# Delta-net stage of a hybrid trunk: later key and value transposes, pair scales on VectorE, E blocks fixed ahead of the KQ copies on GpSimd

## The chip, the cores and the metric

The kernel runs on one core of a Trainium2 chip. The metric is the device time of one execution in microseconds; the median of several runs is quoted. One execution was taken by the hardware profiler, and all rows below are from it. TensorE multiplies, VectorE (DVE), ScalarE (ACT) and GpSimd (POOL) do the rest, and SyncE's queue (SP) loads the weights.

## The reference

Two layers on x of 256 tokens by 1024, each h + ½·FFN_a, h + mixer, h + ½·FFN_b, with an RMSNorm before and behind each part. The mixer of layer 0 is a short gated convolution. That of layer 1 is a gated delta-net, cut to what matters here:

```
qkv, z, b, a = split(x @ w_in)
qkv = silu(causal_conv(qkv, conv_w))       # width 4, each channel by itself
q, k, v = split(qkv)                       # 8 key heads, 16 value heads of 128
q, k = l2norm(q), l2norm(k); beta = sigmoid(b)
g = -exp(a_log) * softplus(a + dt_bias)    # per head and token, then cumsum in a chunk of 64
a_ = strict_lower(k_beta @ k.T * decay)    # per chunk
t_inv = inverse(eye + a_)                  # unit lower triangular
u = t_inv @ v_beta; w = t_inv @ (k_beta * exp(g))
# over the chunks: v_new = u - w @ state; o = q_g @ state + qk @ v_new; the state is updated
o = rms_norm(o) * norm_w * silu(z);  y = o @ w_out
```

## The kernel before, in words

The 256 tokens are two tiles of 128. The kernel is a stream of weight units of 128x1024: each is loaded by SyncE into one of three buffers (raw), split on ScalarE into a high part (whi, `unit`, L119) and on VectorE into a low part (wlo, L121), eight of each in a pool, and used by three matmuls per product (high by high, high by low, low by high). Results of the projections go to four PSUM banks named mm; four others (acc) serve the small products. TensorE takes its instructions in program order. Work that isn't a projection lies in generators ("chains"). A ticker resumes them: every group of 24 matmuls of a projection (`stat_group`, two to a bank, for keys and values; `act_group`, one to a bank, for z) calls `tk.tick()` two or four times, and a chain that yields n is resumed n ticks later. So the constants KQ_WAIT, INV_WAIT, V_WAIT set where in the stream of matmuls a step of a chain is placed. The order on the other engines is made by the scheduler from the program, per engine and fixed; `tc.issue_after` pins an instruction behind another.

The delta-net stage (`gdn_proj`, about 690 to 880 us of the profile) goes so:

- The head slabs: gates a and b, and the first seven of the 16 key and query columns. `gates` (L530 to L537) makes beta, the log decay and its sums; `decays` makes the decay matrices (dec) with exponentials on ScalarE and masks on GpSimd (L559).
- The other columns of keys and queries. `conv` (L583) is one ScalarE operation that reads the bank, and three VectorE operations that read it again; `kq_raw` and `kq_silu` follow, then, one group of two key heads after the other, `kq_chain`: transposes on TensorE (L618), a copy, products KQ (L621), sums of squares (junk, kss, L630), scales (rk, dsc, nk, eq), KQ times its decay (L645), and copies of its 32x32 blocks into blk (L652).
- `invert`: a transpose on VectorE (L669), 62 small VectorE operations (L677, L679; they grow from 31 to 256 columns and shrink again), two more transposes (L681, L683). GpSimd copies the results into KQ (L689, 32 copies) and E (L699, L700), and TensorE puts the blocks together (L707 to L739).
- Three z groups (`z_group`, a bank per tile, then a SiLU into zs that empties it, L573), and four value groups, each of two pairs (`v_pair`): a bank of two heads, `conv` into yb, SiLU, a wait of V_WAIT ticks, transposes (L757) into another mm bank, scaled copies nv (L759). The last z group, the scan over the chunks and the output projection follow.

The order of the projections, and the pair's chain:

```
        for gi in range(NG - 1):
            z_group(gi)
        for gi in range(NG):
            v_group(gi)
        z_group(NG - 1)
```

Of the kernel before, what the change touches and what calls it, by code (L numbers as in the profile page):

```python
# [7 lines left out]
F32 = mybir.dt.float32  # L8
F32R = mybir.dt.float32r
AF = mybir.ActivationFunctionType  # L10
ALU = mybir.AluOpType
PSUM = bass.MemoryType.PSUM

P = 128
T = 256
NT = 2
# [5 lines left out]
NG = 4  # L22
# [7 lines left out]
NSMALL = 22  # L30
NBIG = 8
NROW = 3
KQ_WAIT = 3
INV_WAIT = 37
V_WAIT = 4
SCAN_WAIT = 2
ORD = "00111222"
GORD = "00012222"
# [11 lines left out]
def trunk_kernel(ctx: ExitStack, tc: tile.TileContext, x, norm_g, w_gu, w_dn, sc_in, sc_cw, sc_out,  # L50
# [425 lines left out]
    def gdn_proj(xh, xl, mid):  # L476
# [30 lines left out]
        def gates():  # L507
            def sm(name):
                return sp.tile([P, NT, NVH], F32, name=name, bufs=1)

            a, u, e, z, q = sm("ga"), sm("gb"), sm("gc"), sm("gd"), sm("ge")
            G.tensor_tensor(a, ba[:, :, NVH:], bc(dtb, NT), ALU.add)
            G.tensor_scalar(u, a, 0.0, -2.0, ALU.max, ALU.mult)
            G.tensor_tensor(e, a, u, ALU.add)
            first = S.activation(e, e, AF.Exp).ins
            with tc.issue_after(first):
                S.activation(al, al, AF.Exp)
            S.activation(beta, ba[:, :, 0:NVH], AF.Exp, scale=-1.0)

            V.tensor_scalar(z, e, 2.0, None, ALU.add)  # L520
            V.reciprocal(z, z)
            V.tensor_tensor(z, z, e, ALU.mult)
            V.tensor_tensor(u, z, z, ALU.mult)
            V.tensor_scalar(q, u, 1.0 / 19.0, None, ALU.mult)
            for k in (17, 15, 13, 11, 9, 7, 5, 3):
                V.scalar_tensor_tensor(q, q, 1.0 / k, u, ALU.add, ALU.mult)
            V.scalar_tensor_tensor(q, q, 1.0, z, ALU.add, ALU.mult)
            V.tensor_scalar(a, a, 0.0, None, ALU.max)
            V.scalar_tensor_tensor(q, q, 2.0, a, ALU.mult, ALU.add)
            V.scalar_tensor_tensor(g, q, -1.0, bc(al, NT), ALU.mult, ALU.mult)  # L530
            G.tensor_scalar(beta, beta, 1.0, None, ALU.add)
            V.reciprocal(beta, beta)
            pg = side_bank().rearrange("p a b -> p (a b)")[:, 0:2 * NVH].rearrange("p (t n) -> p t n", t=NT)
            PE.matmul(pg[:, 0, :], lhsT=tri_s, rhs=g[:, 0, :], start=True, stop=True)
            PE.matmul(pg[:, 1, :], lhsT=tri_u, rhs=g[:, 1, :], start=True, stop=True)
            S.activation(etail, pg[:, 0, :], AF.Exp)
            S.activation(eg, pg[:, 1, :], AF.Exp)  # L537

        def decays():
# [10 lines left out]
                gus.append(gu)  # L550
            while not convs:
                yield 1
            for gi in range(NG):
                for t in range(NT):
                    pd = side_bank()
# [30 lines left out]
                V.scalar_tensor_tensor(dst[:, j:], src[:, 0:T - j], cw[:, ch, 3 - j:4 - j],  # L586
                                       dst[:, j:], ALU.mult, ALU.add)

        raws, kq_time = {}, [0] * KD

        def kq_raw(kh, c, src):
            if kh not in raws:
                raws[kh] = slab([P, 2, T], F32, "kq")
            conv(raws[kh][:, c, :], src, c * KD + kh)
            if c == 1:
                if dec_done[0]:
                    kq_silu(kh, raws[kh])
                else:
                    convs.append((kh, raws[kh]))
# [5 lines left out]
        def kq_chain():  # L605

            for gi in range(NG):
# [23 lines left out]
                    yield 1  # L631
                while dec[1][gi] is None:
                    yield 1
                G.tensor_scalar(ss, ss, EPS, None, ALU.add)
                rk = sp.tile([P, NT, 2], F32, name="rk", bufs=2)
                V.reciprocal(rk, ss[:, :, 0, :])
                dd = small(f"dsc{gi}", 8).rearrange("p (t n) -> p t n", t=NT)
                for t in range(NT):
                    G.tensor_tensor(dd[:, t, :].rearrange("p (k v) -> p k v", k=2),
                                    beta[:, t, 4 * gi:4 * gi + 4].rearrange("p (k v) -> p k v", k=2),  # L640
                                    rk[:, t, :].unsqueeze(2).broadcast_to([P, 2, 2]), ALU.mult)
                for t in range(NT):
# [14 lines left out]
                w = small(f"wt{gi}", 4)  # L657
                G.tensor_tensor(w, etail[:, 4 * gi:4 * gi + 4], dd[:, 0, :], ALU.mult)
                Dsc[gi], nk[gi], eq[gi], wt[gi] = dd, n, q, w
                yield 1  # L660
            tk.start(invert())


# [3 lines left out]
        def invert():  # L667
# [14 lines left out]
            Yd = row("blk").rearrange("p (a b) -> p a b", a=B32)  # L682
            V.transpose(Yd.rearrange("p h i -> p i h"), X)  # L683
            T1 = row("blk").rearrange("p (a b) -> p a b", a=B32)
            for gi in range(NG):
                for t in range(NT):
                    for b in range(4):
                        r = slice(b * B32, (b + 1) * B32)
                        G.tensor_copy(KQ[gi][t][r, :, 0, r], Yd[r, 8 * gi + t:8 * gi + t + 7:2, :])  # L689
            yield INV_WAIT  # L690
            for half in range(2):
                hs = slice(16 * half, 16 * half + 16)
                gis = (2 * half, 2 * half + 1)
                E = {}
                for gi in gis:
                    E[gi] = slab([P, 8, 64], F32, "E64")
                    for b in range(2):
                        r = slice(b * B32, (b + 1) * B32)
                        G.tensor_copy(E[gi][r, :, r], Xd[r, 8 * gi:8 * gi + 8, :])  # L699
                    G.memset(E[gi][0:B32, :, B32:], 0.0)  # L700
                pt = side_bank().rearrange("p a (b c) -> p (a b) c", c=B32)
                for x in range(16):
                    ht = 16 * half + x
# [44 lines left out]
        def v_pair(gi, i, pt, tiles):  # L748
# [1 line left out]
            for j in range(2):  # L750
                conv(vc[:, j, :], pt[:, j, :], 16 + 4 * gi + 2 * i + j)
            silu(vc, vc)
            yield V_WAIT
            tp = ps.tile([P, NT, 2, P], F32, name="mm")
            for t in range(NT):
                for j in range(2):
# [134 lines left out]
        def head_tail(late):  # L891
            yield 1
            late()
            for kh, c in order[0:7]:
                kq_raw(kh, c, craw[kh][:, c, :])

        tk.start(head_tail(head_slabs([load_slab(gdn_h0, GSPLIT, GORD), load_slab(gdn_h1, GSPLIT, GORD[4:])], xh, xl, evac_head, mid, 0)))
# [158 lines left out]
```

## Time and profile before

| | us |
|---|---|
| runs, lowest, median, highest | 1125.82, 1127.42, 1130.31 |
| the profiled execution | 1128.42 |
| its span, first to last instruction | 1126.5 |
| TensorE busy in it | 1100.2 (98%) |
| VectorE, ScalarE, GpSimd busy | 749.9, 651.8, 88.8 |
| mean granted TensorE clock | 0.995 |

Busy time is the time in which an engine has an instruction under way; waits are what is left of the span. A start in the timeline counts from the span's beginning. Where an engine was idle before an instruction, the row says for how long and which instruction, of which engine and line, released it.

### The profile page before, as it was taken

How to read it: one execution, taken by the hardware profiler on the slowest of the kernel's cores; microseconds unless marked ns; L12 is line 12 of the kernel's file. 1: busy time of each engine (PE TensorE's matmuls, PEld its weight loads, DVE VectorE, ACT ScalarE, POOL GpSimd, SP SyncE). 2: the span in 40 equal slices, each digit the busy share in tenths (PEclk: the TensorE clock that was granted, in tenths of full speed). 3: DMA queues.
4: the chain of work that ended last, by engine and by line, in shares of the span. 5: the costliest groups of instructions: out<-in, count | busy, mean ns of one | idle time of the engine just before them, and what ended most of it. 6: DMA issues, size and time to landing. Idle time of an engine off the chain costs nothing.

```text
span 1126.5 us, 16842 instructions
## 1 busy us (share of the span) xinstructions
PE 1100.2 (98%) x6284; PEld 942.4 (84%) x6284; DVE 749.9 (67%) x1140; ACT 651.8 (58%) x1201; POOL 88.8 (8%) x167
## 2 busy tenths in 40 slices
PE   9999999999999999999999999889899999999997
PEld 6888887888788888788888877778899887888886
DVE  7776735687777663577765468768946557767543
ACT  6666535545556653556664358784587645666432
POOL 0100000000200000010000012110141212000000
PEclk9999999999999999999999999999999999999999
DMA  8755555656566565576555653327332355655552
GB/s 271 244 185 190 191 166 167 225 180 198 182 223 204 171 206 165 163 229 209 189 185 169 193 185 113 94 94 227 114 129 76 131 168 168 213 199 190 185 168 75
DMA packets 55955, 198.12 MB, mean 176 GB/s; under 512 B 6721, under 2 KB 7233, under 8 KB 55874
## 3 DMA queue, kind: packets, MB, share of 16 engines
q1 hardware_dynamic: 55728, 196.99, 54.2%
q8 instruction: 49, 0.80, 0.3%
q14 instruction: 32, 0.26, 0.1%
q10 hardware_dynamic: 146, 0.07, 0.0%
HBM read 195.99 MB, written 1.05 MB: 175 GB/s over the span
## 4 chain that ended last, share of the span: by engine, by line
PE 81%; DVE 7%; ACT 5%; DMA 3%; issue 2%; POOL 2%; SPq 0%; DVEq 0%; POOLq 0%; ACTq 0%
PE mm L298 27%; PE mm L301 14%; PE acc L324 7%; PE acc L325 7%; PE acc L323 7%; PE mm L221 3%; PE mm L222 3%; PE mm L225 3%; DVE wlo L121 2%; ACT whi L119 1%; ACT blk L652 1%; DVE kq L586 1%; PE mm L176 1%; ACT junk L147 1%; DMA raw<-in_w_gu 1%
## 5 line engine op out<-in xcount | busy, mean ns | idle before, releaser
L121 DVE TENSOR_TENSOR wlo<-raw,whi 128x1024 fp32r<-128x1024 f32 (+2 forms) x362 | 437.5, 1220 | 240.2 <-ACT whi L119 201.5
L119 ACT ACTIVATE whi<-raw 128x1024 fp32r<-128x1024 f32 (+2 forms) x362 | 376.1, 1051 | 224.3 <-PE acc L325 104.6
L298 PE MATMUL mm<-x,whi 128*128 128x512 f32 x1312 | 329.4, 393 | 0.0
L298 PEld LDWEIGHTS mm<-x,whi 128*128 128x128 f32 x1312 | 235.9, 189 | 42.4
L301 PEld LDWEIGHTS mm<-x,wlo 128*128 128x128 f32 x1312 | 179.0, 190 | 12.8
L301 PE MATMUL mm<-x,wlo 128*128 128x256 f32 x1312 | 182.9, 282 | 0.0
L323 PE MATMUL acc<-whi,hb 128*128 128x512 f32 x352 | 136.5, 388 | 0.0
L324 PE MATMUL acc<-wlo,hb 128*128 128x512 f32 x352 | 135.6, 385 | 0.3 <-DVE wlo L121 0.3
L325 PE MATMUL acc<-whi,hb 128*128 128x512 f32 x352 | 135.3, 385 | 0.0
L308 ACT ACTIVATE corr<-mm 128x256 f32<-128x256 f32 x164 | 61.2, 376 | 67.4 <-PE mm L301 65.6
L221 PE MATMUL mm<-whi,x 128*128 128x512 f32 (+1 forms) x240 | 94.4, 394 | 0.9 <-ACT x L178 0.7
L222 PE MATMUL mm<-wlo,x 128*128 128x512 f32 (+1 forms) x240 | 94.2, 393 | 0.7 <-DVE wlo L121 0.7
L225 PE MATMUL mm<-whi,x 128*128 128x512 f32 (+1 forms) x240 | 87.8, 389 | 0.2 <-DVE x L179 0.2
L324 PEld LDWEIGHTS acc<-wlo,hb 128*128 128x128 f32 x352 | 66.2, 188 | 13.8 <-DVE wlo L121 0.8
L323 PEld LDWEIGHTS acc<-whi,hb 128*128 128x128 f32 x352 | 66.2, 188 | 13.1
L325 PEld LDWEIGHTS acc<-whi,hb 128*128 128x128 f32 x352 | 66.1, 188 | 13.2
L154 POOL TENSOR_SCALAR rstd<-ss 128x1 f32<-128x1 f32 x24 | 12.3, 513 | 786.1 <-ACT junk L147 786.1
L278 PE MATMUL mm<-x,whi 128*128 128x256 f32 x200 | 59.7, 299 | 2.0 <-DVE kq L586 2.0
L279 PE MATMUL mm<-x,whi 128*128 128x256 f32 x200 | 58.4, 292 | 0.0
L280 PE MATMUL mm<-x,wlo 128*128 128x256 f32 x200 | 57.9, 289 | 0.0
L222 PEld LDWEIGHTS mm<-wlo,x 128*128 128x128 f32 x240 | 45.2, 188 | 11.2 <-DVE wlo L121 2.9
L221 PEld LDWEIGHTS mm<-whi,x 128*128 128x128 f32 x240 | 45.2, 188 | 11.1 <-ACT x L178 2.7
(216 smaller groups left out, 1238.3 us busy)
## 6 DMA issues: line engine op xcount, KB each, us to landing
raw<-in_w_gu SPq DMA_DIRECT2D x176, 512.0 KB, 4.2
raw<-in_w_dn SPq DMA_DIRECT2D x88, 512.0 KB, 3.6
raw<-in_sc_in SPq DMA_DIRECT2D x24, 512.0 KB, 4.1
raw<-in_gdn_z SPq DMA_DIRECT2D x16, 512.0 KB, 3.9
raw<-in_gdn_v SPq DMA_DIRECT2D x16, 512.0 KB, 4.2
raw<-in_gdn_out SPq DMA_DIRECT2D x16, 512.0 KB, 3.7
gamma<-in_norm_g SPq DMA_DIRECT2D x11, 512.0 KB, 5.4
raw<-in_gdn_a SPq DMA_DIRECT2D x9, 512.0 KB, 4.4
```

The costliest lines, as they stand in the source:

```text
L119: S.activation(hi[:, r], raw[:, r], AF.Copy)
L121: newest[0] = V.tensor_tensor(lo[:, r], raw[:, r], hi[:, r], ALU.subtract).ins
L221: PE.matmul(pt, lhsT=xh[:, t, k, :], rhs=hi, start=(k == 0), stop=False)
L222: PE.matmul(pt, lhsT=xh[:, t, k, :], rhs=lo, start=False, stop=False)
L225: PE.matmul(pt, lhsT=xl[:, t, j, :], rhs=part(j)[0], start=False, stop=(j == KD - 1))
L278: PE.matmul(ptile, lhsT=hi, rhs=h2, start=(k == 0), stop=False)
L298: PE.matmul(flat, lhsT=part(k, 0), rhs=xx[:, k].rearrange("p h t q -> p (h t q)"), start=(k == 0), stop=False)
L301: PE.matmul(flat[:, T:], lhsT=part(k, 1), rhs=xx[:, k, 0].rearrange("p t q -> p (t q)"), start=False, stop=(k == KD - 1))
L308: S.activation(c, pt[:, 1, :], AF.Copy)
L323: PE.matmul(o, lhsT=yh(c, t), rhs=hi[:, r], start=(c == 0), stop=False)
L324: PE.matmul(o, lhsT=yh(c, t), rhs=lo[:, r], start=False, stop=False)
L325: i = PE.matmul(o, lhsT=yl(c, t), rhs=hi[:, r], start=False, stop=(c == n - 1)).ins
```

## The change

Names and numbers only: KQ_WAIT goes from 3 to 5 ticks, the wait behind a key pair from 1 to 3 (PAIR_WAIT), V_WAIT from 4 to 9, 6, 4, 4 by value group, and the head's seven convolutions are issued four and then, three ticks later, three (CONV_WAIT). `kq_raw` counts the two parts of a key head in place of waiting for the second column. The sums of the gates (two matmuls, two exponentials) move from `gates` into `decays`, behind the first convolutions. The EPS addition and the scale dsc go from GpSimd to VectorE. In `invert`, `place(half)` issues for each half the E copies and zeros and then 16 KQ copies, in an order that is pinned; the second half is placed later.

```
-KQ_WAIT = 3
+KQ_WAIT = 5
+PAIR_WAIT = 3
-V_WAIT = 4
+V_WAIT = (9, 6, 4, 4)
+CONV_WAIT = 3
...
+        def gate_sums():
             pg = side_bank().rearrange("p a b -> p (a b)")[:, 0:2 * NVH].rearrange("p (t n) -> p t n", t=NT)
...
             while not convs:
                 yield 1
+            gate_sums()
...
             conv(raws[kh][:, c, :], src, c * KD + kh)
-            if c == 1:
+            parts[kh] += 1
+            if parts[kh] == 2:
...
-                G.tensor_scalar(ss, ss, EPS, None, ALU.add)
+                V.tensor_scalar(ss, ss, EPS, None, ALU.add)
...
-                    G.tensor_tensor(dd[:, t, :].rearrange("p (k v) -> p k v", k=2),
+                    V.tensor_tensor(dd[:, t, :].rearrange("p (k v) -> p k v", k=2),
...
-                yield 1
+                yield PAIR_WAIT
             tk.start(invert())
...
-            for gi in range(NG):
-                for t in range(NT):
-                    for b in range(4):
+            E, placed = {}, [None]
+
+            def place(half):
+
+                gis = (2 * half, 2 * half + 1)
+                for gi in gis:
+                    E[gi] = slab([P, 8, 64], F32, "E64")
+                    for b in range(2):
                         r = slice(b * B32, (b + 1) * B32)
-                        G.tensor_copy(KQ[gi][t][r, :, 0, r], Yd[r, 8 * gi + t:8 * gi + t + 7:2, :])
+                        with tc.issue_after(placed[0]) if placed[0] else nullcontext():
+                            G.tensor_copy(E[gi][r, :, r], Xd[r, 8 * gi:8 * gi + 8, :])
+                    with tc.issue_after(placed[0]) if placed[0] else nullcontext():
+                        last = G.memset(E[gi][0:B32, :, B32:], 0.0).ins
+                placed[0] = last
+                for gi in gis:
+                    for t in range(NT):
+                        for b in range(4):
+                            r = slice(b * B32, (b + 1) * B32)
+                            with tc.issue_after(placed[0]):
+                                last = G.tensor_copy(KQ[gi][t][r, :, 0, r], Yd[r, 8 * gi + t:8 * gi + t + 7:2, :]).ins
+                placed[0] = last
+
+            place(0)
             yield INV_WAIT
...
-                E = {}
-                for gi in gis:
-                    E[gi] = slab([P, 8, 64], F32, "E64")
...
+                if half:
+                    place(1)
...
             silu(vc, vc)
-            yield V_WAIT
+            yield V_WAIT[gi]
...
-            for kh, c in order[0:7]:
+            for i, (kh, c) in enumerate(order[0:7]):
+                if i == 4:
+                    yield CONV_WAIT
                 kq_raw(kh, c, craw[kh][:, c, :])
```

How the instructions stand, at three places. Numbers behind a name tell buffers apart; line numbers of the change are its own (SiLU L578 for L573, conv L589 and L591 for L584 and L586, projections L280 for L278).

ScalarE, from the last copies of the keys' blocks to the second value pair. Before (zs is the SiLU of a z bank, yb a value pair):

```order
L652 ACTIVATE blk_6238<-KQ_7222 32x4x32 x3
L119 ACTIVATE whi_7481<-raw_7479 128x1024 [waits DMAHW4_49,PE_49]
...
L573 ACTIVATE zs_7450<-mm_7425 128x512 [waits PE_49]
...
L573 ACTIVATE zs_7477<-mm_7452 128x512 [waits PE_49]
...
L573 ACTIVATE zs_7528<-mm_7503 128x512 [waits PE_49]
...
L573 ACTIVATE zs_7555<-mm_7530 128x512 [waits PE_49]
L119 ACTIVATE whi_7711<-raw_7709 128x1024 [waits DMAHW7_49,DVE_49]
L584 ACTIVATE yb_7645<-mm_7583,gcw_6224 128x256 [waits PE_49]
L584 ACTIVATE yb_7645<-mm_7583,gcw_6224 128x256 [waits DVE_49]
```

In the change:

```order
L658 ACTIVATE blk_6238<-KQ_7282 32x4x32 x3
L121 ACTIVATE whi_7563<-raw_7561 128x1024 [waits DMAHW2_49,PE_49]
...
L589 ACTIVATE yb_7637<-mm_7575,gcw_6224 128x256 [waits PE_49]
L589 ACTIVATE yb_7637<-mm_7575,gcw_6224 128x256 [waits DVE_49]
L578 ACTIVATE yb_7637<-yb_7637 128x512 [waits DVE_49,Activation_49]
...
L589 ACTIVATE yb_7722<-mm_7624,gcw_6224 128x256 [waits PE_49]
L589 ACTIVATE yb_7722<-mm_7624,gcw_6224 128x256 [waits DVE_49]
L121 ACTIVATE whi_7854<-raw_7852 128x1024 [waits DMAHW3_49]
L578 ACTIVATE yb_7722<-yb_7722 128x512 [waits DVE_49,Activation_49]
L578 ACTIVATE zs_7469<-mm_7317 128x512
L578 ACTIVATE zs_7520<-mm_7495 128x512
L578 ACTIVATE zs_7547<-mm_7522 128x512
```

Three zs operations moved from ahead of the first value convolution to behind the SiLU of the second pair; and the last copies into blk stand behind six more weight units.

TensorE, the first matmul of each of the first three value banks. Before:

```order
L278 MATMUL mm_7583<-x2_5783,whi_7559 128x256 [waits Activation_49]
...
L278 MATMUL mm_7632<-x2_5783,whi_7559 128x256 [waits PE_49]
...
L278 MATMUL mm_7717<-x2_5783,whi_7693 128x256 [waits Activation_49]
...
L757 MATMUL mm_7730<-ident_81,yb_7645 128x128 [waits PE_49,Activation_49]
```

In the change:

```order
L280 MATMUL mm_7575<-x2_5783,whi_7551 128x256 [waits Activation_49]
...
L280 MATMUL mm_7624<-x2_5783,whi_7551 128x256 [waits DVE_49,Activation_49]
...
L280 MATMUL mm_7709<-x2_5783,whi_7685 128x256 [waits DVE_49,Activation_49]
...
L280 MATMUL mm_7768<-x2_5783,whi_7685 128x256 [waits PE_49,Activation_49]
...
L776 MATMUL mm_7803<-ident_81,yb_7637 128x128 [waits PE_49,Activation_49]
```

The second and third bank now wait for VectorE as well; the first transposes moved from the third bank's matmuls into the fourth's.

VectorE in the change, ahead of the end of the first value convolution (28 operations of the inversion and six splits stand between the first two rows):

```order
L675 STREAM_TRANSPOSE blk_7324<-blk_6238 128x1024 [waits Activation_49]
...
L591 SCALAR_TENSOR_TENSOR yb_7637<-mm_7575,gcw_6224,yb_7637 128x255 [waits Activation_49]
L683 TENSOR_TENSOR sg_7371<-blk_7324,blk_7326 128x255 [waits DVE_49]
...
L591 SCALAR_TENSOR_TENSOR yb_7637<-mm_7575,gcw_6224,yb_7637 128x253 [waits DVE_49]
L683 TENSOR_TENSOR sg_7380<-blk_7324,blk_7326 128x252 [waits DVE_49]
...
L123 TENSOR_TENSOR wlo_7843<-raw_7840,whi_7842 128x1024 [waits DMAHW1_49,PE_49,Activation_49]
L683 TENSOR_TENSOR sg_7407<-blk_7324,blk_7326 128x135 [waits DVE_49]
L591 SCALAR_TENSOR_TENSOR yb_7722<-mm_7624,gcw_6224,yb_7722 128x255 [waits Activation_49]
```

Before, 37 operations of the inversion stood ahead of the first value convolution; between the two convolutions stand 19 of them now, and two splits.

## Rows read from the trace of the kernel before

**Rows 1.** The page, TensorE's and the other engines' busy time.

```profile
PE 1100.2 (98%) x6284; PEld 942.4 (84%) x6284; DVE 749.9 (67%) x1140; ACT 651.8 (58%) x1201; POOL 88.8 (8%) x167
```

**Rows 2.** Windows: length; busy PE, PEld, DVE, ACT, POOL; granted clock, DMA share, GB/s.

```profile
700.00:750.00 50.00, 42.18 (x264) 37.55 (x263) 37.83 (x76) 41.99 (x131) 10.04 (x25) 0.93 0.27 86
750.00:800.00 50.00, 46.41 (x264) 41.06 (x264) 43.56 (x88) 28.22 (x39) 3.02 (x8) 0.97 0.55 168
```

**Rows 3.** TensorE's waits: us in total, times, longest.

```profile
PE acc L618 <- ACT kq L573: 3.6, 2, 3.1
...
PE mm L757 <- ACT yb L573: 3.4, 1, 3.4
PE mm L278 <- DVE kq L586: 2.0, 1, 2.0
PE acc L621 <- DVE KQ L645: 1.7, 1, 1.7
```

**Rows 4.** A window of 5 us around one of the longest idle times, same columns.

```profile
745.00:750.00 5.00, 3.31 (x10) 2.85 (x11) 2.57 (x4) 3.67 (x16) 0.25 (x2) 0.66 0.71 220
```

**Rows 5.** Windows of the key stage and of the inversion, same columns.

```profile
697.00:758.00 61.00, 53.18 (x306) 45.49 (x305) 45.31 (x89) 50.99 (x147) 16.06 (x35) 0.94 0.26 81
758.00:810.00 52.00, 48.41 (x313) 44.45 (x313) 48.21 (x102) 28.38 (x39) 0.00 (x0) 0.97 0.57 176
```

**Rows 6.** Timeline of GpSimd: start, duration, operation, idle before and releaser.

```profile
727.28 0.25 POOL L634 TENSOR_SCALAR kss<-kss 128x8 f32<-128x8 f32 x1 [7.33 <-ACT junk L630]
...
729.06 0.35 POOL L639 TENSOR_TENSOR dsc<-beta,rk 128x4 f32<-128x4 f32 x2
...
815.44 12.48 POOL L689 COPY KQ<-blk 32x128 f32<-32x128 f32 x32
```

**Rows 7.** Timeline of ScalarE, last key copies to first value pair.

```profile
753.34 1.85 ACT L652 ACTIVATE blk<-KQ 32x128 f32<-32x128 f32 x4 [0.82 <-DVE KQ L645]
...
768.41 1.06 ACT L119 ACTIVATE whi<-raw 128x1024 fp32r<-128x1024 f32 x1 [1.51 <-DMA raw<-in_gdn_v]
...
782.83 0.58 ACT L573 ACTIVATE zs<-mm 128x512 f32<-128x512 f32 x1
...
785.43 0.46 ACT L584 ACTIVATE yb<-mm,gcw 128x256 f32<-128x256 f32 x1
```

**Rows 8.** Timeline of VectorE, from the inversion's first transpose through the first value convolution.

```profile
758.02 1.25 DVE L669 STREAM_TRANSPOSE blk<-blk 128x1024 f32<-128x1024 f32 x1 [2.01 <-ACT blk L652]
...
777.88 0.41 DVE L677 TENSOR_TENSOR sg<-blk 128x240 f32<-128x240 f32 x1
778.32 0.41 DVE L679 TENSOR_TENSOR blk<-blk,sg 128x240 f32<-128x240 f32 x1
...
789.32 0.48 DVE L586 SCALAR_TENSOR_TENSOR yb<-mm,gcw,yb 128x255 f32<-128x255 f32 x1
...
793.28 0.47 DVE L586 SCALAR_TENSOR_TENSOR yb<-mm,gcw,yb 128x253 f32<-128x253 f32 x1
```

**Rows 9.** VectorE's groups from 760.2 to 782.8: busy, mean ns, idle before.

```profile
L121 DVE TENSOR_TENSOR wlo<-raw,whi 128x1024 fp32r<-128x1024 f32 x11 | 13.4, 1217 | 1.7 <-ACT whi L119 1.5
L679 DVE TENSOR_TENSOR blk<-blk,sg 128x31 f32<-128x31 f32 (+13 forms) x14 | 4.7, 333 | 0.3
L677 DVE TENSOR_TENSOR sg<-blk 128x31 f32<-128x31 f32 (+13 forms) x14 | 4.6, 330 | 0.2
```

**Rows 10.** The same from 788.0 to 802.1, steps of the inversion alone.

```profile
L679 DVE TENSOR_TENSOR blk<-blk,sg 128x255 f32<-128x255 f32 (+9 forms) x10 | 3.8, 375 | 0.1
L677 DVE TENSOR_TENSOR sg<-blk 128x252 f32<-128x252 f32 (+9 forms) x10 | 3.6, 364 | 0.1
```

**Rows 11.** Timeline of TensorE, start of the first value bank.

```profile
778.01 0.28 PE L278 MATMUL mm<-x,whi 128*128 128x256 f32 x1
778.12 0.28 PE L279 MATMUL mm<-x,whi 128*128 128x256 f32 x1
```

**Rows 12.** The same, the first value transposes.

```profile
794.53 1.12 PE L757 MATMUL mm<-ident,yb 128*128 128x128 f32 x4 [3.41 <-ACT yb L573]
```

More of the change, by code (lines that the diff above doesn't have):

```diff
@@ L587, in conv @@
                                        dst[:, j:], ALU.mult, ALU.add)
-        raws, kq_time = {}, [0] * KD
+        raws, kq_time, parts = {}, [0] * KD, [0] * KD
         def kq_raw(kh, c, src):
@@ L693, in invert @@
                 gis = (2 * half, 2 * half + 1)
-                E = {}
-                for gi in gis:
-                    E[gi] = slab([P, 8, 64], F32, "E64")
[L697 to L700, printed above, removed]
+                if half:
+                    place(1)
                 pt = side_bank().rearrange("p a (b c) -> p (a b) c", c=B32)
```

## The prediction

> **What bounds the kernel now.** I read the page first: TensorE is busy 1100.2 us of a span of 1126.5, 98% [rows 1], so a change that leaves its matmuls alone can win only what TensorE loses, and costs what it makes TensorE wait. Where it loses, the windows of 50 us tell: in the delta-net stage it is busy 42.18 us from 700 to 750 and 46.41 from 750 to 800 [rows 2], 11.4 us short in all. The list of waits names the losers there [rows 3]: key transposes waiting for the SiLU of a key pair (L618, 3.6 us), the KQ products (L621, 1.7), the first projection after the heads, which waits for a bank that a convolution still reads (L278, 2.0), the first value transposes (L757, 3.4). [...]
>
> The other engines have room on average, but not everywhere: VectorE is busy 48.21 us of the 52 between 758 and 810 [rows 5], where it runs the 62 steps of the inversion between splits of weights and convolutions of values. My forecast rests on its queue in that stretch.
>
> **The change, part by part.**
>
> *Key transposes later* (KQ_WAIT, PAIR_WAIT), *head convolutions in two parts*, *gate sums behind the convolutions*. They push the key chain back, so that SiLU and squares are done when TensorE arrives. At best this removes the waits of L618 and L621, 3.6 + 1.7 = 5.3 us [rows 3], and the 1.7 us of low clock [rows 4]; at worst nothing. I take the best. The wait of L278 I leave in: a convolution of the head still has to empty its bank, from the same queue.
>
> *The scales on VectorE.* Four additions (0.25 us) and four pairs of products (0.35) leave GpSimd [rows 6]. On VectorE I take 0.2 us for each of the 12, half a step of the inversion [rows 8], 2.4 us in all, in a stretch in which VectorE is idle for 61.0 − 45.3 = 15.7 us [rows 5]. In return the products no longer stand in GpSimd's queue until 1.8 us behind the addition (727.28, 729.06 [rows 6]); KQ can be scaled some 1.2 us sooner. That is part of what removes the L621 wait, and isn't counted twice. If VectorE were full there, it would cost 2.4 us.
>
> *E blocks ahead of the KQ copies.* The 32 copies take 12.48 us from 815.44 [rows 6]. Putting the E blocks ahead and halving the copies lets the first half of the blocks go some 6 us sooner, but no large wait of TensorE names GpSimd as its releaser [rows 3]. I book nothing; if TensorE reached the blocks sooner than now, up to those 6 us could show, but by the working below it gets there later.
>
> *The first value transposes later* (V_WAIT 9 in place of 4). Those of the first pair stand 12 matmuls into the third value bank and wait 3.41 us there [rows 12]. Nine ticks put them into the fourth bank: −3.4.
>
> So far there are only gains. **Now what the moves do to the queues.** On ScalarE, each SiLU of a z bank (zs, L573) stands among the weight splits now, and its bank is free at once: the last runs at 782.83, the first value convolution at 785.43 [rows 7]. In the change the SiLUs of the last three z banks stand behind the convolutions of two value pairs and the SiLU of the second. There are four such banks. Three stay held by z, so the second value pair must go into the bank of the first, and the third pair into it again; the order shows TensorE waiting for VectorE and ScalarE at both, which it doesn't now. Each of the two waits ends with the last convolution operation of the pair before, and those stand in VectorE's queue in the midst of the inversion.
>
> First wait. VectorE has, from the inversion's first transpose to the end of that convolution: the transpose, 1.2 [rows 8]; 28 steps, 4.7 + 4.6 = 9.3 [rows 9], plus 0.04 from each to the next (777.88, 778.32 [rows 8]), 10.4; six splits at 1.22 less 0.08 that lies beside the next operation, 6.8 [rows 9]; six convolution operations with steps of the inversion between them, 4.4 (789.32 to 793.75 [rows 8]). Sum 22.8 us. When does the transpose start? Now at 758.02, released by the last copy into blk on ScalarE [rows 8]. In the change six more splits and two more SiLUs stand ahead of that copy on ScalarE: 6 × 1.06 + 2 × 0.58 = 7.5 [rows 7], less 0.2 for starts that overlap, 7.3. ScalarE is busy 51.0 of the 61 us there [rows 5]: the ends are 755.3 (all its 10 us of idle time filled) and 765.3 (none). I take 764.5, since only the 0.82 us ahead of the copies at 753.34 [rows 7] is idle time that a split moved ahead fills for certain; the rest are waits within the key chain, which is moved back, not shortened. The convolution then ends at 787.3.
>
> TensorE would now be ready for that bank at 783.8 (778.01 and 48 matmuls at 0.12 [rows 11]), and with the 5.3 us gained at 778.5. So it waits until 787.4: +8.9 us, which uses up what the key chain gained.
>
> Second wait. From there VectorE has 19 steps, 19/20 of 3.8 + 3.6, 7.0 [rows 10], and 0.04 after each, 0.8; two splits, 2.3; the second convolution with another split in it, 4.8, by the first's 4.4 with shorter steps. That is about 15.0 us, against the 5.8 of matmuls in which TensorE doesn't wait. The third bank starts at 802.4, where it starts at 789.6 now: +9.2.
>
> What follows is as now, less the 3.4 us; I let the low clock that follows the L757 wait follow this one.
>
> **Sum:** −5.3 + 8.9 + 9.2 − 3.4 = **+9.4 us**; the 1.7 us of clock only lengthen the first wait, so they don't count. The profiled execution took 1128.42 us (its span of 1126.5 and 1.9 around it), so it would be 1137.8. It lies 1.0 above the median: **1136.8 us**, 0.8% more.
>
> On banks, the rows show that the step from the first value bank to the next costs nothing now: TensorE's list has no wait there [rows 3]. [...]
>
> On the scales, the rows show 0.18 us a product on GpSimd [rows 6]. [...]
>
> **The rivals.**
>
> *A. The inversion starts early and the waits shrink (20%).* ScalarE fills its idle time in the key stage, the transpose starts at 755.3 to 759, and each microsecond comes off the sum: 9.4 − 9.2 = +0.2 at 755.3, +3.9 at 759. That is 1127.6 to 1131.3, no measurable change. For it: ScalarE idles 10 us there. Against it: most of that waits for the chain that the change moves back.
>
> *B. The banks don't bind (7%).* If VectorE has done the second convolution when TensorE is ready for the third bank, at 778.5 + 5.8 = 784.3, neither wait exists and the gains stand: −5.3 − 1.7 − 3.4 = −10.4, 1117; with half of them, 1122. This is the mechanism on the other side; it decides where the first transpose starts before 784.3 − 15.0 − 22.8 = 746.5. Against it: the last copies into blk but four start at 753.34 now [rows 7], and their place is later in the change. It also comes about if the convolutions end sooner than by my count of the queue.
>
> *C. Worse (15%, all slower).* Weights come slowly: at 768.41 a split on ScalarE waits 1.51 us for a value slab [rows 7], and a late split on VectorE holds the steps and convolutions behind it. With six splits ahead of the first convolution and three ahead of the end of the second, two to four such waits add 3 to 6 us: 1139.8 to 1142.8.
>
> *The change does less than it says.* If L618 and L621 still wait, TensorE comes later to the second bank and waits less there: the end is the same, since VectorE sets it. So this shares the forecast's time.
>
> **How the numbers follow.** A measurement of this kernel can tell about 0.5%, 5.6 us, from no change: faster is below 1121.8, slower above 1133.1. The forecast (58%) and C make 73%, of which some 3% lie below 1133.1 (a transpose before 760.8). So slower 0.70, same 0.23, faster 0.07. The range goes from A's end, 1127, to C's, 1143.
>
> **What would show it.** Right: the second and third value bank each begin after 7 to 11 us of idle TensorE, released by the yb convolution on VectorE, with a granted clock well below 1 behind; no wait at the value transposes; small ones at the key transposes; the inversion's first transpose at 762 to 766; three zs SiLUs behind the second yb SiLU; KQ copies in two groups of 16. Wrong: no idle time at these two places, or a first transpose before 757. If the two waits are there but make less than 12 us, VectorE's queue was shorter than I counted.

## The result, and the profile after

The changed kernel took 1137.77 us (median of 4 runs, 1137.27 to 1139.30) against 1128.87 for the kernel before on the same chip: ratio 1.0083, 95% interval 1.0054 to 1.0112. That is 8.9 us more; the prediction had named 9.4 us more and 1136.8 us. The profiled execution took 1139.3 us with a span of 1137.6, 11.1 above that of before.

TensorE's waits after, the four largest of the stage (line numbers are the change's own):

```profile
PE mm L280 <- DVE yb L591: 10.2, 1, 10.2
PE mm L280 <- DVE blk L685: 6.8, 1, 6.8
...
PE mm L280 <- DVE kq L591: 2.6, 2, 2.0
...
PE acc L627 <- ACT junk L636: 0.9, 1, 0.9
```

Against [rows 3]: the waits of the key transposes (3.6) are gone, that of the KQ products is 0.9 in place of 1.7 (and is for the squares now), the value transposes' 3.4 is gone. Two new ones make 17.0 us, both on the first matmul of a value bank. The timeline of TensorE has them at the second and third bank:

```profile
789.35 0.55 PE L280 MATMUL mm<-x,whi 128*128 128x256 f32 x1 [10.20 <-DVE yb L591]
...
803.57 0.55 PE L280 MATMUL mm<-x,whi 128*128 128x256 f32 x1 [6.82 <-DVE blk L685]
```

VectorE, from the inversion's first transpose to the end of the second value convolution (compare [rows 8]):

```profile
766.98 1.25 DVE L675 STREAM_TRANSPOSE blk<-blk 128x1024 f32<-128x1024 f32 x1 [0.51 <-ACT blk L658]
...
784.65 0.48 DVE L591 SCALAR_TENSOR_TENSOR yb<-mm,gcw,yb 128x255 f32<-128x255 f32 x1
...
788.73 0.47 DVE L591 SCALAR_TENSOR_TENSOR yb<-mm,gcw,yb 128x253 f32<-128x253 f32 x1
...
802.95 0.48 DVE L591 SCALAR_TENSOR_TENSOR yb<-mm,gcw,yb 128x253 f32<-128x253 f32 x1
803.34 0.21 DVE L685 TENSOR_TENSOR blk<-blk,sg 128x60 f32<-128x60 f32 x1
```

The first convolution ends at 789.20 and the second bank starts at 789.35; the second ends at 803.43 and the third bank starts at 803.57. For the latter the wait list names the inversion step (L685), which merely ended last before the start; by the program it is the convolution's last operation that frees the bank, and the start lies 0.14 us behind its end, as that of the second bank lies 0.15 behind the first's. ScalarE shows the rest of the chain:

```profile
797.37 0.45 ACT L589 ACTIVATE yb<-mm,gcw 128x256 f32<-128x256 f32 x1
...
803.52 0.63 ACT L578 ACTIVATE yb<-yb 128x512 f32<-128x512 f32 x1 [1.43 <-DVE yb L591]
804.05 1.55 ACT L578 ACTIVATE zs<-mm 128x512 f32<-128x512 f32 x3
```

The three z banks, the last of them full since about 773, are emptied at 804.05, behind the second pair's SiLU. The windows of 50 us (columns as in [rows 2]) say where the loss lies:

```profile
700.00:750.00 50.00, 46.47 (x287) 40.91 (x286) 42.28 (x90) 41.97 (x118) 9.62 (x16) 0.97 0.33 106
750.00:800.00 50.00, 36.55 (x202) 32.19 (x200) 43.15 (x91) 25.88 (x51) 2.79 (x6) 0.89 0.47 146
```

From 700 to 750 TensorE is busy 4.3 us longer than before; then 9.9 less.

### The profile page after: what moved, and what is told of

Read it like the earlier page. It is cut to its first block, busy times and chain, and to the rows that moved or that the text cites. A ratio compares the mean times of both kernels' runs of the same rounds, so it can differ in the third digit from the quotient of the medians.

```text
span 1137.6 us, 16862 instructions
## 1 busy us (share of the span) xinstructions
PE 1101.4 (97%) x6284; PEld 945.2 (83%) x6284; DVE 754.4 (66%) x1152; ACT 651.3 (57%) x1201; POOL 84.6 (7%) x155
## 4 chain that ended last, share of the span: by engine, by line
PE 81%; DVE 7%; ACT 5%; issue 3%; DMA 2%; POOL 1%; SPq 0%; DVEq 0%; POOLq 0%; ACTq 0%
PE mm L300 27%; PE mm L303 14%; PE acc L326 7%; PE acc L327 7%; PE acc L325 7%; PE mm L223 3%; PE mm L224 3%; PE mm L227 3%; DVE wlo L123 2%; PE mm L280 2%; PE mm L281 2%; PE mm L282 2%; ACT whi L121 1%; ACT blk L658 1%; DMA raw<-in_w_gu 1%
## 5 line engine op out<-in xcount | busy, mean ns | idle before, releaser
L300 PEld LDWEIGHTS mm<-x,whi 128*128 128x128 f32 x1312 | 235.9, 189 | 42.2
L303 PEld LDWEIGHTS mm<-x,wlo 128*128 128x128 f32 x1312 | 179.0, 190 | 12.8
L223 PE MATMUL mm<-whi,x 128*128 128x512 f32 (+1 forms) x240 | 96.7, 403 | 1.9 <-ACT x L180 1.8
L227 PE MATMUL mm<-whi,x 128*128 128x512 f32 (+1 forms) x240 | 88.3, 390 | 0.0
L280 PE MATMUL mm<-x,whi 128*128 128x256 f32 x200 | 61.7, 308 | 19.6 <-DVE yb L591 10.2
L281 PE MATMUL mm<-x,whi 128*128 128x256 f32 x200 | 59.2, 296 | 0.0
L280 PEld LDWEIGHTS mm<-x,whi 128*128 128x128 f32 x200 | 40.9, 205 | 21.2 <-issue 17.6
```

What stands on the lines that cost most here:

```text
L223: PE.matmul(pt, lhsT=xh[:, t, k, :], rhs=hi, start=(k == 0), stop=False)
L227: PE.matmul(pt, lhsT=xl[:, t, j, :], rhs=part(j)[0], start=False, stop=(j == KD - 1))
L280: PE.matmul(ptile, lhsT=hi, rhs=h2, start=(k == 0), stop=False)
L300: PE.matmul(flat, lhsT=part(k, 0), rhs=xx[:, k].rearrange("p h t q -> p (h t q)"), start=(k == 0), stop=False)
L303: PE.matmul(flat[:, T:], lhsT=part(k, 1), rhs=xx[:, k, 0].rearrange("p t q -> p (t q)"), start=False, stop=(k == KD - 1))
```

## The experiments

All ratios are to the kernel before on the same chip and in the same job. e1 to e4, e5 to e8 and e9 to e11 are three such jobs; runs are compared by their ratios, and what stands behind "give or take" is worked out from the two 95% intervals. The first four runs ask which part made the two waits.

**e1, without the placement.** The GpSimd part of `invert` as before, all else as in the change:

```
-            place(0)
+            for gi in range(NG):
+                for t in range(NT):
+                    for b in range(4):
...
+                        G.tensor_copy(KQ[gi][t][r, :, 0, r], Yd[r, 8 * gi + t:8 * gi + t + 7:2, :])
             yield INV_WAIT
```

> The changed kernel with the inversion's GpSimd part as before (32 KQ copies, then the E blocks half by half, nothing pinned); the key waits, the value waits, the scales on VectorE, the gate sums and the split head convolutions stay. In the built order the three late zs SiLUs now stand ahead of the first value convolution, and the second and third value bank wait for TensorE or ScalarE alone. Theory (the pinned E and KQ copies drew the inversion ahead on VectorE and pushed the zs SiLUs back, and this alone made the two bank waits): the waits of 10.2 and 6.8 us are gone, and with them the low clock behind them, some 3 us; a wait of 1 to 2 us may come at the fifth value bank: 1117 to 1121 us. Rival (the later keys and their later inversion make the waits, whatever GpSimd does): two waits of some 7 to 10 us stay, 1133 to 1138.

Measured: 1137.35 us, ratio 1.0062 (1.0038 to 1.0086). The waits went as expected, and the time didn't. TensorE's waits, GpSimd's timeline and 5 us windows of e1:

```profile
PE acc L738 <- POOL E L706: 7.0, 1, 7.0
...
PE mm L763 <- ACT yb L578: 3.4, 1, 3.4
...
PE mm L280 <- DVE yb L591: 1.1, 1, 1.1
```

```profile
816.92 14.36 POOL L695 COPY KQ<-blk 32x128 f32<-32x128 f32 x32 [55.19 <-DVE blk L689]
831.34 0.82 POOL L705 COPY E<-blk 32x256 f32<-32x256 f32 x2
832.20 0.30 POOL L706 MEMSET E<- 32x256 f32 x1
```

```profile
830.00:835.00 5.00, 2.44 (x18) 2.33 (x19) 0.00 (x0) 0.44 (x1) 4.35 (x13) 0.57 0.00 0
835.00:840.00 5.00, 5.00 (x33) 4.43 (x32) 1.20 (x3) 1.84 (x4) 1.08 (x3) 0.50 0.00 0
840.00:845.00 5.00, 5.00 (x95) 4.82 (x93) 1.47 (x2) 2.23 (x5) 0.00 (x0) 0.50 0.01 3
845.00:850.00 5.00, 5.00 (x119) 4.83 (x118) 1.45 (x3) 2.87 (x7) 0.00 (x0) 0.72 0.37 108
```

Without the placement the E blocks stand behind 14.36 us of KQ copies, the block products wait 7.0 us for them, and behind that wait, from 832.56, the granted clock is near 0.50 until about 848 (TensorE's 128x256 products start 0.21 us apart up to 847.78, and 0.11 to 0.12 behind). By these windows my estimate of the loss is 0.50 × 2.44 + (0.50 + 0.50 + 0.28) × 5 = 7.6 us. So the placement made the bank waits, and it also removes a wait that the later keys bring (GpSimd starts at 816.92, before at 815.44). In time the two come out alike: the ratios of e1 and of the change, 1.0062 and 1.0083, have intervals that overlap.

**e2, the placement alone** in the kernel before:

```
+            place(0)
             yield INV_WAIT
...
+                if half:
+                    place(1)
```

> The kernel before with the pinned placement of E and KQ copies alone. In the built order all value convolutions now stand behind the whole inversion and its two last transposes on VectorE. Theory (the placement reorders VectorE): the first value convolution ends near 758 + 1.2 + 23 (62 steps) + 10 (nine splits) + 4 (two transposes) + 5 (four more splits) + 3 = 804 to 805, so the first value transposes wait some 14 us in place of 3.4: 1137 to 1141. Rival (the placement concerns GpSimd alone, off the path): 1127 to 1130.

Measured: 1148.72 us, ratio 1.0164 (1.0143 to 1.0184), worse than I expected. TensorE's waits:

```profile
PE acc L720 <- DVE blk L681: 23.3, 1, 23.3
```

The value convolutions did move behind the inversion, but the wait fell elsewhere: on TensorE the block products now stand ahead of the products of the last z bank (from 797.73), and so of all value banks (the first at 804.72), and wait until 795.88 for the inversion's second transpose, 23.3 us. TensorE's order is the scheduler's too, not only the program's, as I had told it ahead of the prediction. The rival is out: the placement isn't a matter of GpSimd alone.

**e3, z SiLUs pinned ahead** of the value convolutions, in the change:

```
-                silu(zs, pt.rearrange("p (h d) -> p h d", h=4))
+                zlast[0] = silu(zs, pt.rearrange("p (h d) -> p h d", h=4))
...
-                conv(vc[:, j, :], pt[:, j, :], 16 + 4 * gi + 2 * i + j)
+                with tc.issue_after(zlast[0]):
+                    conv(vc[:, j, :], pt[:, j, :], 16 + 4 * gi + 2 * i + j)
```

> The changed kernel with one more pin: a value pair's convolution is issued only behind the SiLU of the z group before it, so the three zs SiLUs stand ahead of it on ScalarE and free their banks. In the built order the second and third value bank no longer wait for VectorE, but the value convolutions now stand behind the whole inversion. Theory (held banks are what TensorE waited for at these two places): both waits go, and one takes their place where the first value transposes come, 24 matmuls into the fourth bank: TensorE there at 794, the convolution done at 767 + 1.2 + 23 + 7 + 4 + 3 = 805 to 806, so some 12 us in place of 17, and one low stretch of clock less: 1130 to 1134. Rival (TensorE waited for the weights or for VectorE's splits, and the bank is incidental): waits at the same two places, 1136 to 1139. If neither wait is replaced: 1118.

Measured: 1140.75 us, ratio 1.0093 (1.0074 to 1.0112). TensorE's waits and ScalarE's timeline:

```profile
PE acc L726 <- DVE blk L687: 20.7, 1, 20.7
```

```profile
779.39 1.55 ACT L578 ACTIVATE zs<-mm 128x512 f32<-128x512 f32 x3
```

With the banks emptied at 779.39, both bank waits are gone. One wait takes their place, but at the block products, as in e2, and 20.7 us long. They stand ahead of the second value bank here, so TensorE comes to that bank only at 800.51; it starts it then, though the first value convolution ends at 803.9. So a bank that z has left needs no convolution to end; the fuller test of held banks is e5. The pin freed the banks and cost as much elsewhere; what had tied the z SiLUs to the end of the inversion was still to be found.

**e4, the tick counts alone** in the kernel before:

```
-KQ_WAIT = 3
+KQ_WAIT = 5
+PAIR_WAIT = 3
-V_WAIT = 4
+V_WAIT = (9, 6, 4, 4)
```

> The kernel before with the changed tick counts alone (keys 5 and 3, values 9, 6, 4, 4). Theory (the later transposes are sound and win what the prediction gave them, 5.3 + 3.4 us and up to 3.4 of clock): 1117 to 1122, and the waits at the key transposes and the first value transposes are below 1 us each. Rival (VectorE, whose inversion starts later, sets the end anyway and the transposes wait as before): 1127 to 1132.

Measured: 1140.44 us, ratio 1.0093 (1.0070 to 1.0116): a miss.

```profile
PE acc L733 <- POOL E L701: 6.9, 1, 6.9
PE mm L279 <- DVE yb L587: 3.9, 1, 3.9
```

The waits of the key transposes are at most 1.0 us, as expected, but there is a wait for E as in e1, a wait of 3.9 us at the fifth value bank, and a mean granted clock of 0.75 from 800 to 850. The inversion ends later: GpSimd, released by its last transpose, begins its KQ copies at 817.98 (815.44 before), and the E blocks stand behind 14.20 us of them. So the later keys and values cost some 10 us by themselves in the kernel before, by other waits than the change's.

The next two runs ask what ties the z SiLUs to the inversion; the five behind them give a price to parts of the change. The E blocks and zs come from the same pool of 22 SBUF slabs. In the change the second E slab is first written, in the order of the program, by a copy that needs the finished inverse, and the last three zs come behind it in the program. (So is the first E slab, whose zeros GpSimd nonetheless wrote early, at 760.77; why only the second was held up, no row shows.)

**e5, the zeros first.** The whole change, with the two memsets ahead of the four copies:

```
                 for gi in gis:
                     E[gi] = slab([P, 8, 64], F32, "E64")
+                    with tc.issue_after(placed[0]) if placed[0] else nullcontext():
+                        G.memset(E[gi][0:B32, :, B32:], 0.0)
+                for gi in gis:
                     for b in range(2):
...
-                            G.tensor_copy(E[gi][r, :, r], Xd[r, 8 * gi:8 * gi + 8, :])
-                    with tc.issue_after(placed[0]) if placed[0] else nullcontext():
-                        last = G.memset(E[gi][0:B32, :, B32:], 0.0).ins
+                            last = G.tensor_copy(E[gi][r, :, r], Xd[r, 8 * gi:8 * gi + 8, :]).ins
```

> The changed kernel with two lines in another order: in the pinned placement the two memsets that write zeros into the E blocks come ahead of the four E copies. Every other part of the change stays. New theory: the E blocks share a pool of 22 SBUF slabs with zs, and slabs are given out in the order of the program; in the change the first touch of the second E slab was a copy that needs the finished inverse, so the three z slabs that come after it in the program were not given out before the inversion's end, and their SiLUs stood behind it, with their banks. A memset needs nothing, so both E slabs are given out early. In the built order the zs SiLUs are ahead of the value convolutions again, and the value banks wait for none of them. Expected: the bank waits of 10.2 and 6.8 us gone; waits of 1.1 and 3.4 us as without the placement (e1); the 7.0 us wait for E there gone too, and with it most of the low clock behind it, since E and half the KQ copies are done some 6 us sooner: 1121 to 1130 us. Rival (the pins, not the slabs, drew the inversion ahead): 1136 to 1139.

Measured: 1124.74 us (median of 10), ratio 0.9949 (0.9936 to 0.9963), faster than both kernels, and 1.3% below the change. TensorE's waits, a window of it, ScalarE's timeline and GpSimd's:

```profile
PE mm L777 <- ACT yb L578: 3.5, 1, 3.5
PE mm L280 <- DVE kq L591: 2.6, 2, 2.0
...
PE mm L280 <- DVE yb L591: 1.2, 1, 1.2
```

```profile
785.00:790.00 5.00, 5.00 (x44) 5.00 (x43) 4.97 (x14) 3.17 (x4) 0.00 (x0) 1.00 0.05 19
```

```profile
768.12 0.58 ACT L578 ACTIVATE zs<-mm 128x512 f32<-128x512 f32 x1
769.67 0.58 ACT L578 ACTIVATE zs<-mm 128x512 f32<-128x512 f32 x1
777.33 0.58 ACT L578 ACTIVATE zs<-mm 128x512 f32<-128x512 f32 x1
```

```profile
760.96 0.56 POOL L699 MEMSET E<- 32x256 f32 x2
...
815.78 1.73 POOL L704 COPY E<-blk 32x256 f32<-32x256 f32 x4 [53.15 <-DVE blk L687]
817.74 8.12 POOL L711 COPY KQ<-blk 32x128 f32<-32x128 f32 x16 [0.23 <-DVE blk L689]
```

VectorE's queue is as late as in the change (the inversion's first transpose at 767.16, the first value convolution done at 789.42), but the z banks are empty by 777.91, and TensorE goes through the second and third value bank without a stop (5.00 us busy from 785 to 790, where the change has 0.65). So held banks were what TensorE waited for. The KQ copies are still pinned behind E; the first touch of the slab moved, and with it the instruction that this pin names, now the last E copy in place of the last memset. No run here parts these two. In the change GpSimd wrote zeros into one E slab ahead of the inversion, the other waited:

```profile
760.77 0.30 POOL L703 MEMSET E<- 32x256 f32 x1
761.03 0.94 POOL L677 MEMSET blk<- 128x1024 f32 x1
...
807.28 1.72 POOL L701 COPY E<-blk 32x256 f32<-32x256 f32 x4 [45.09 <-DVE blk L687]
809.04 0.30 POOL L703 MEMSET E<- 32x256 f32 x1
```

**e6, the placement alone, zeros first,** in the kernel before: e2 with the edit of e5.

> The kernel before with the placement alone, its memsets first. Theory (slabs): the 23 us wait of e2 is gone, and the time is that of the kernel before, 1126 to 1131, since GpSimd's copies are off the path there. Rival (the pinned order itself costs): 1137 to 1149 as in e2.

Measured: 1130.12 us, ratio 1.0003 (0.9989 to 1.0017). The 23.3 us wait is gone; the rival is out. With early keys the placement is worth nothing, as the prediction had booked it.

**e7 and e8, the key waits** with the zeros first. e7 sets KQ_WAIT to 3 and PAIR_WAIT to 1, e8 leaves 5 and sets PAIR_WAIT to 1:

```
-KQ_WAIT = 5
-PAIR_WAIT = 3
+KQ_WAIT = 3
+PAIR_WAIT = 1
```

> The memsets first, and the key waits as before (3 and 1); value waits, scales on VectorE, gate sums, split head convolutions and placement stay. Theory (the later keys start the inversion 9 us later, and that makes the waits of 1.1 and 3.4 us that are left in e5): the inversion starts at 757 to 759, the waits at the value transposes are below 1 us, the waits at the key transposes are as before (about 4 us with the low clock): 1119 to 1124, below e5 by 1 to 5. Rival (the later keys pay, as the prediction had it): e5 is faster than this by 3 to 5 us.

> The memsets first, the wait ahead of each key transpose 5 ticks as in the change, the wait behind a pair 1 tick as before. Theory: the SiLU waits of the key transposes go as in the change, and the inversion starts only 2 to 4 us later than before: the best of the set, 1117 to 1122. Rival (any later key costs as much as it wins): as e7 or slower.

Measured: e7 1126.86 us, ratio 0.9970 (0.9958 to 0.9982); e8 1129.25, 0.9993 (0.9979 to 1.0008). In e7 the inversion starts at 762.28, not at 758, the KQ products wait 2.5 us, and a wait of 2.4 at the value transposes stays: the theory fell. The rival has the direction: the later keys pay 0.0021 of 1130, 2.4 us, give or take 2.0, where it had 3 to 5. e8 missed its 1117 to 1122 as well, and both counts are needed: there the KQ products wait 4.2 us for the squares and the value transposes 4.1, though the inversion starts at 758.92.

**e9, the third and fourth pair later** (9, 8, 5, 4), as e5 otherwise:

```
-V_WAIT = (9, 6, 4, 4)
+V_WAIT = (9, 8, 5, 4)
```

> As e5 (memsets first, all parts of the change), with value waits of 9, 8, 5, 4 ticks in place of 9, 6, 4, 4: the third pair's transposes, which wait 3.5 us for their SiLU in e5, come 20 matmuls later, the fourth's some 20. Theory (what is left in e5 is a transpose placed ahead of a late convolution, so a later place wins its wait and the low clock behind it): 3.5 + 1.7 us below e5, 1118.5 to 1121.5. Rival (VectorE sets the end of this stretch, so a later place only moves the wait to the fifth or sixth value bank or to the blocks): 1123 to 1126.

Measured: 1123.50 us, ratio 0.9952 (0.9937 to 0.9967), the same as e5 within the intervals. The 3.5 us wait is gone, and in its place stand small ones at the same stretch's blocks and transposes (1.3 us for blk, 0.7 for the inversion's transpose, 0.6 for nv). That is what the rival had: the wait moves, and VectorE sets the end: the inversion's transpose releases the block products at 815.51 here, and GpSimd's E copies at 815.78 in e5.

**e10, the value waits at 4,** and **e11, the scales on GpSimd,** each as e5 otherwise:

```
-V_WAIT = (9, 6, 4, 4)
+V_WAIT = (4, 4, 4, 4)
```

```
-                V.tensor_scalar(ss, ss, EPS, None, ALU.add)
+                G.tensor_scalar(ss, ss, EPS, None, ALU.add)
...
-                    V.tensor_tensor(dd[:, t, :].rearrange("p (k v) -> p k v", k=2),
+                    G.tensor_tensor(dd[:, t, :].rearrange("p (k v) -> p k v", k=2),
```

> As e5, with the value waits at 4 as before. This prices the value waits with the banks free. Theory (the inversion starts at 767, the first value convolution ends near 788.5 and its SiLU at 790; the first transposes are reached 12 matmuls into the third bank, at 786): a wait of about 4 us there, and 2 to 4 more at the second and third pair, less the 3.5 of e5, and low clock behind them: 1127 to 1132. Rival (VectorE sets the end, wherever the transposes stand): 1123 to 1126.

> As e5, with the EPS addition and the scale dsc back on GpSimd. Prediction's term: KQ can be scaled some 1.2 us later in each group, of which the waits of the KQ products (L627, 1.0 us in e5) and of the banks behind show a part: 0.5 to 2.5 us above e5, 1125 to 1127.5; the inversion starts up to 1.2 us later. Rival (off the path on either engine): within 0.5 us of e5.

Measured: e10 1129.54 us (its ten runs from 1124.59 to 1131.48), ratio 0.9988 (0.9968 to 1.0007); e11 1128.42, 0.9990 (0.9975 to 1.0005). Against e5 the value waits are worth 0.0039 of 1130, 4.4 us, give or take 2.7, and the scales 0.0041, 4.6 us, give or take 2.3, where 0.5 to 2.5 were expected. In e11 the inversion starts at 769.53 (767.16 in e5), the fifth value bank waits 3.9 us in place of 1.2, and VectorE waits for the scale:

```profile
763.18 3.23 DVE L651 SCALAR_TENSOR_TENSOR KQ<-acc,dsc,dec 128x256 f32<-128x256 f32 x8 [1.53 <-POOL dsc L645]
```

## Why the prediction was right

**The two bank waits.** This is the step that carried it. Forecast 8.9 and 9.2 us beyond the start of now; measured: the second bank starts at 789.35 (forecast 787.4), the third at 803.57 (802.4). Taken apart, the inversion starts at 766.98, later than the 764.5 that I took and than the 765.3 that I held for the end of the range. ScalarE's idle time up to there did not shrink (10.35 us of the 70 from 697 to 767, against 10.0 of 61), and my sum of splits on ScalarE is not the whole way by which the start moved. The last key group shows it, TensorE's transposes, the last square and the first scaled KQ, before

```profile
746.69 1.12 PE L618 MATMUL acc<-ident,kq 128*128 128x128 f32 x4 [3.06 <-ACT kq L573]
749.39 0.19 ACT L630 ACTIVATION_READ_ACCUMULATOR junk<-acc 128x1 f32 x1
751.65 3.23 DVE L645 SCALAR_TENSOR_TENSOR KQ<-acc,dsc,dec 128x256 f32<-128x256 f32 x8 [1.53 <-POOL dsc L639]
```

and in the change:

```profile
750.13 0.60 PE L624 MATMUL acc<-ident,kq 128*128 128x128 f32 x4
757.83 0.20 ACT L636 ACTIVATION_READ_ACCUMULATOR junk<-acc 128x1 f32 x1
760.60 3.23 DVE L651 SCALAR_TENSOR_TENSOR KQ<-acc,dsc,dec 128x256 f32<-128x256 f32 x8
```

The transposes are placed 3.4 us later, the squares end 8.4 us later, since copies into blk, splits and a z SiLU stand ahead of and among them on ScalarE, and KQ is scaled 8.95 us later. From there to the inversion nothing is added: ScalarE's splits behind the squares lie in its wait for KQ, 1.87 us of which is left.

From the inversion's start to the end of the convolution VectorE took 22.2 us (forecast 22.8), and from that to the second convolution's end 14.2 (15.0). A start 2.5 us too late and two stretches 0.6 and 0.8 us too short leave the third bank 1.2 us late. TensorE was ready at 779.15 (forecast 778.5).

Two of the signs that I had named were missed by a little: the second wait is 6.82 us, where I had 7 to 11, and the first transpose lies behind 762 to 766. Rival C, slow weights, does not show on VectorE: ScalarE waits for value slabs, up to 2.22 us at a time, but VectorE is busy 35.08 of the 36.45 us from 766.98 to 803.43.

**The key chain.** The waits of L618 went, and 0.9 us at L621 stayed in place of 1.7, so about 4.4 of 5.3 us came; as foretold, it only lengthened the first bank wait. The 1.7 us of low clock that the forecast sets beside them is an estimate, 0.34 × 5 us from the mean granted clock in [rows 4]; the change has 1.00 from 745 to 750. **The value transposes'** 3.4 us went. **The clock** cost more than I let it: 5 us windows of the change

```profile
785.00:790.00 5.00, 0.65 (x3) 0.68 (x4) 4.92 (x14) 1.10 (x2) 0.00 (x0) 0.50 0.02 7
790.00:795.00 5.00, 5.00 (x34) 5.00 (x34) 4.60 (x12) 0.49 (x1) 0.00 (x0) 0.74 0.01 3
...
800.00:805.00 5.00, 1.43 (x7) 1.46 (x8) 4.96 (x14) 3.01 (x5) 0.00 (x0) 0.50 0.73 229
805.00:810.00 5.00, 5.00 (x26) 5.00 (x26) 4.04 (x3) 0.61 (x2) 2.43 (x7) 0.54 0.35 105
```

give 0.50 × 1.4 + 0.46 × 5 = 3.0 us lost behind the third bank's wait, as an estimate: busy time by what the granted clock lacks of 1. The 128x256 products there start 0.21 us apart from 804 to 809, at 0.50, and 0.12 from 810 on, at 1.00. Behind the L757 wait, whose low clock I had let stand for it, it is 0.30 × 5.47 = 1.6 us in the kernel before:

```profile
794.53:800.00 5.47, 5.47 (x34) 5.47 (x35) 5.47 (x14) 3.52 (x6) 0.00 (x0) 0.70 0.36 104
```

The sum in measured terms: third bank 803.57 − 789.5 = 14.0, less 3.4, plus 1.4 of clock, less the 0.6 of the small waits at the blocks that went, 11.4; the spans of the two profiled executions differ by 11.1. Since the prediction's sum was made for the span, 9.4 was 1.7 us too little there, and that the medians differ by 8.9, so near to it, is in part luck.

**What the prediction had wrong, though the sum held.** The two bank waits came as foretold, but "I book nothing" for the placement, right for the kernel before with the zeros first (e6), is wrong for the change: without the placement the two waits are not there (e1), and its memset's place caused the order that I had read from ScalarE's queue without asking where it came from. Nor did I see that later keys and values without it cost as much, by the wait for E (e1, e4). The likely way is that slabs are handed out in the order of the program, so that a slab whose first writer waits for the inverse holds up the zs behind it; e2, e3, e5 and e6 fit it, and e5 differs from the change only in the place of the memsets and in the instruction that the pin names; the handing out itself is seen in no row, so this last step is argued, not shown. Rival B, free banks with all gains, was priced at 1117; in e5 the banks are free, by another way than B's, and it came to 1124.74. By e9's rows, VectorE still sets the stretch behind. The scales, booked at nothing beyond their share of L621, are worth 4.6 us with the banks free (e11).

On banks, the traces show 10.20 and 6.82 us of waiting where three of the four banks were held, no wait at these two places where they weren't, and 1.2 us at the fifth bank (e5). There are four in e5 too, so they were not too few, but held too long. That an SBUF slab stood behind it is the account above.

On the scales, a product pair took 0.23 to 0.24 us on VectorE,

```profile
760.40 0.23 DVE L645 TENSOR_TENSOR dsc<-beta,rk 128x4 f32<-128x4 f32 x2
```

against 0.35 on GpSimd [rows 6], a factor of 1.5. That is not the point: in GpSimd's queue dsc stands behind nk (1.04 us) and eq (0.24) in the kernel before, and VectorE waits 1.53 us for it in e11 as in the kernel before, where the pair itself takes 0.35.

## What to carry to other kernels

Read a change's effect on queues from the built order, then find out which line made that order: the part to blame may be a harmless one, here a memset that stood two lines too late. Where a tile shares a pool with urgent tiles, let its first instruction in the program be one that waits for nothing; that is what e5 did (ratio 0.9949, where the change has 1.0083). And price each part with the others in place: the E placement is worth nothing in the kernel before (e6), and, with the zeros first, 0.0113 of 1130, 12.8 us, give or take 3.1, once the keys and values come later (e1 against e5).

## What the hardware showed that I had not expected

The stretch of low granted clock was of very different length behind two waits of like length. After the 6.82 us wait of the change the granted clock was 0.50 for some 6 us, until about 809.5, and by my estimate 3.0 us were lost, with 128x256 products behind the wait; after the 3.41 us wait of [rows 12] the loss was 1.6 us by the same estimate (0.70 over 5.47 us), with four transposes and the same products. After the 7.0 us wait of e1 the granted clock stayed near 0.50 for some 15 us, in which TensorE had an instruction under way all the time: block products of 64x64 and 32x32, 33 and 95 instructions in the windows from 835 and from 840, with 128x256 products between them. There the clock cost more (7.6 us, estimated) than the wait. No run here varied alone what TensorE does behind the wait, so the reason stays open.
